# Scratch copies issued from ScalarE's queue, sub-norm rows made by TensorE transposes, zero-padded queries written by GpSimd, small buffers as rings inside one tile

## The chip, the cores and the metric

The kernel runs on one core of a Trainium2 chip. The metric is device time in microseconds of one launch, the median of several runs. Before the change it is 1522.74 us (three runs, 1522.72 to 1524.1).

## What is computed

Two decoder layers over 1040 tokens (16 learned ones and 1024 of the input) of width 1024, in float32. One projection gives the inputs of two groups of attention heads: four differential heads (two softmaxes of 64-wide rotated queries and keys, the second subtracted with a factor, a 128-wide value, then an RMS norm over those 128 channels) and eight forgetting heads (a running sum of log-sigmoids is added to the scores). Both are gated and go through an output projection.

```python
u = rms_norm(h, norm_g)
proj = jnp.einsum('bld,dp->blp', u, w_in)            # dq dk dv dz fq fk fv fz f_logit
...
p = probs(qa, k1) - lam * probs(qc, k2)              # differential heads, q and k after rope
o_a = rms_norm(einsum(p, v_a), subln_g) * (1.0 - lambda_init)
...
s = einsum(q, k_f) * f_scale + c_q - cum             # forgetting heads
mixed = concatenate([o_a * silu(dz), o_b * silu(fz)])
return h + jnp.einsum('blm,md->bld', mixed, w_out)
```

## The kernel before

Every float32 product is made of products of float32r parts: an operand is split into a high part (a cast) and a low part (the rest), and three matmuls stand for one. Token rows are kept transposed in `XTh` and `XTl`, channels on the partitions.

The work of a layer is eight units: units 0 to 3 are the differential heads, units 4 to 7 pairs of forgetting heads. For unit j+1 the program writes `unit_proj` (keys, queries, values; weights are loaded by SyncE, split by GpSimd in `load_w`, L307 and L310, and multiplied at L334) behind `attend` of unit j, and the gates and the norm of unit j behind that. A scheduler then puts each engine's instructions into one fixed order, so that projections of the next unit fill TensorE between the score, transpose and value matmuls of the present one. Each engine, and each engine's DMA queue, works through its list in that order: an instruction that waits holds what stands behind it.

All DMAs are begun by SyncE, through `dma` (L141) and `load_w` (L301). Four kinds matter here:

- the rotary swap: ScalarE writes `raw` out of PSUM (L484), four DMAs copy its 32-row quarters crosswise into `sw`, and VectorE and GpSimd multiply and add (L493 to L495);
- copies of the queries' high part into the other half of the same tile (`qa<-qa`), and of the keys of the forgetting heads (`k<-k`, named k2 in the code);
- the zero-padded low queries of the differential heads: `low_queries` copies 64 rows of `ql` per half and block into `qzs`, two slots behind `XTl` (so the rows name it `XTl<-ql`); it is the stationary operand of the score matmul at L673;
- the norm of the differential heads, `sub_norm`: 1/rms of every token, in `vr`, goes to DRAM (`rr`), comes back broadcast over the partitions (`bc`), and VectorE multiplies the head's output `OT` by it (L901).

Small buffers come from pools (`sm`, and the tags es and ck of `big`). The tile pools are laid out in SBUF by a packer.

Of the kernel before, what the change touches and what calls it, by code (L numbers as in the profile page):

```python
# [12 lines left out]
F32 = mybir.dt.float32  # L13
# [13 lines left out]
NV = 2 * P + 8  # L27
PADC = (272, 544, 1056)
CSW = 1060
LE = max(L, 4 * NV)  # L30
# [4 lines left out]
NE = 4  # L35
ECL = ((272, 4),)
TLS = True
# [14 lines left out]
WLB = 6  # L52
VPB = 2
STB = 3
NQZ = 2
PMB = 4
OTB = 2
CKB2 = 2
Q2B = 2
# [57 lines left out]
def hybrid_kernel(ctx: ExitStack, tc: tile.TileContext, x, meta, norm_g, w_in, b_forget,  # L117
# [40 lines left out]
    def et(name, w=L):  # L158
        for i, (wmax, nb) in enumerate(ECL):
            if w <= wmax:  # L160
                return big.tile([P, wmax], F32, name=name, tag=f"es{i}" if i else "es", bufs=nb or None)
        return big.tile([P, LE], F32, name=name, tag="e", bufs=NE or None)
# [4 lines left out]

    cst = const.tile([P, max(CSW, P + 96 + MW // 2)], F32, name="cst")
    ident = cst[:, 0:P]
# [71 lines left out]
    def rms_stats(hbs, junk, eng):  # L241

        ss = sm.tile([P, 4, 4], F32, name="ss", tag="ss", bufs=3)
# [100 lines left out]
    def load_v01(l):  # L344
# [3 lines left out]
        his, los = room("vwh"), room("vwl")  # L348
        wf = wp.tile([P, KT, 8], F32, name="wf", tag="wf", bufs=1)
        dma(wf, w_in[l, :, 4096:4104].rearrange("(k p) c -> p k c", p=P))  # L350
# [15 lines left out]
    def proj_v01(l, his, los):  # L366
        Vs = [vp.tile([P, NB, 2, P], F32R, name="V", tag="V") for _ in range(2)]
        Vms = [vp.tile([96, 2, P], F32R, name="Vm", bufs=2) for _ in range(2)]
        vpre[l] = (Vs[1], Vms[1])

        mm = big.tile([P, 384], F32R, name="mm", tag="ck", bufs=CKB2 or None).rearrange("p (k c) -> p k c", k=KT)
        nc.gpsimd.memset(mm.bitcast(F32), 0.0)
# [7 lines left out]
        vm = big.tile([P, 384], F32, name="vm", tag="ck", bufs=CKB2 or None)[0:NM, :NV]  # L380
        nc.scalar.copy(vm, ps[32:32 + NM, :NV])
        nc.vector.tensor_tensor(out=vm, in0=ps[0:NM, :NV], in1=vm, op=ALU.add)
        for u in range(2):
# [4 lines left out]
            nc.vector.tensor_tensor(out=Vm[32:32 + NM], in0=x, in1=Vm[0:NM].bitcast(F32), op=ALU.subtract)  # L388
        fn = sm.tile([P, 8, NB], F32, name="fn", tag="fn", bufs=1)
        fm = sm.tile([NM, 8], F32, name="fm", tag="fm", bufs=1)  # L390
        nc.vector.tensor_tensor(out=fm, in0=vm[:, 2 * P:], in1=bfb[0:NM, l], op=ALU.add)
# [22 lines left out]
    def forget(l):  # L414
# [7 lines left out]
        NS = L // 16  # L422
        F = big.tile([P, NM + 2 * P], F32, name="fg", tag="es", bufs=ECL[0][1] or None)
        X, E, T, G = (F[:, i * NS:(i + 1) * NS] for i in range(4))
        off = F[:, 4 * NS:4 * NS + 1]
        tri = big.tile([P, NM + 2 * P], F32, name="tri", tag="es", bufs=ECL[0][1] or None)[:, 0:P]
        tri3 = tri.rearrange("p (a b) -> p a b", b=16)
# [36 lines left out]
    def unit_proj(l, j, U, tabs):  # L464
# [8 lines left out]
        def project(col, chunks, t_lo, scale, split):  # L473
# [9 lines left out]
            def ev(ps, t0, n):  # L483
                nc.scalar.activation(raw[:, t0:t0 + n], ps[:, :n], AF.Copy, scale=scale)  # L484
                todo.append((t0, n))
                if t0 + n < L and len(todo) < RCH:
                    return
                a0, n = todo[0][0], sum(x[1] for x in todo)
                todo.clear()
                c = slice(a0, a0 + n)  # L490
                for a, b in ((0, 32), (32, 0), (64, 96), (96, 64)):
                    dma(sw[a:a + 32, c], raw[b:b + 32, c])
                nc.vector.tensor_tensor(out=raw[:, c], in0=raw[:, c], in1=tabs[0][:, c], op=ALU.mult)  # L493
                nc.gpsimd.tensor_tensor(out=sw[:, c], in0=sw[:, c], in1=tabs[1][:, c], op=ALU.mult)  # L494
                (nc.gpsimd if "a" in ENG else nc.vector).tensor_tensor(out=raw[:, c], in0=raw[:, c], in1=sw[:, c], op=ALU.add)  # L495
                split(raw, a0, 1.0, a0, n)
# [44 lines left out]
        def split_q(src, c0, scale, t0, n):  # L541
# [16 lines left out]
        if not diff and not KE:  # L558
            U.Kb = []
            for m in range(2):  # L560
                k2 = q2t("k2")
                dma(k2[0:64], U.K1[m][halves[m]])
                dma(k2[64:68], augk[:, 2 * (j - 4) + m])
# [13 lines left out]
        V4 = V.rearrange("p b a (c d) -> p b (a c) d", d=64)  # L577
        Vm = vp.tile([96, 2, P], F32R, name="Vm", bufs=2)

        def evv(ps, t0, n):  # L580
            vr = big.tile([P, 384], F32, name="vr", tag="ck", bufs=CKB2 or None)
            nc.scalar.activation(vr[:, :n], ps[:, :n], AF.Copy, scale=1.0 if diff else 0.5)
# [45 lines left out]
    def unit_gate(l, U, from_dram):  # L628
# [9 lines left out]
        def evz(ps, t0, n):  # L638
            gt = big.tile([P, 384], F32, name="gt", tag="ck", bufs=CKB2 or None)
            nc.scalar.activation(gt[:, :n], ps[:, :n], AF.Tanh, scale=0.5)  # L640
# [6 lines left out]
    def low_queries(U, t):  # L647
# [5 lines left out]
        for m in range(2):  # L653
            h = slice(64 * m, 64 * m + 64)
            dma(qz[h, m, :], U.ql[h, t:t + P])
        return [qz[:, m, :] for m in range(2)]

    def scores(U, m, i, low):
# [6 lines left out]
        chs = [(c * n0, n0 if c < nch - 1 else W - c * n0) for c in range(nch)]  # L665
        s = sm.tile([P, 8], F32, name="sst", tag="sst", bufs=SSB or None)
        E = et("E", W)
# [115 lines left out]
    def attend_meta(U):  # L783

        s = sm.tile([P, 8], F32, name="sst", tag="sst", bufs=SSB or None)
        pm2 = ptp.tile([P, 256], F32, name="pm2", tag="pm")[0:16, 0:192].rearrange("p (m c) -> p m c", m=2)
# [28 lines left out]
    def attend(U):  # L815
        U.OT = big.tile([P, L], F32, name="OT", tag="ot", bufs=OTB or None)
        if U.diff:
            U.vr = sm.tile([P, 3, 12], F32, name="vr_", tag="subn", bufs=2)
            if U.l == 0:
# [68 lines left out]
    def sub_norm(U):  # L888
# [84 lines left out]
    for l in range(DEPTH):  # L973
# [59 lines left out]
        if l == 0:  # L1033

            mm = big.tile([P, 384], F32R, name="mm", tag="ck", bufs=CKB2 or None).rearrange("p (k c) -> p k c", k=KT)
            nc.gpsimd.memset(mm.bitcast(F32), 0.0)
# [15 lines left out]
        def out_open(b):  # L1052
# [109 lines left out]
```

## Time and profile before

| | us |
|---|---|
| median of 3 runs | 1522.74 |
| the profiled execution, its own time | 1519.45 |
| its span in the trace | 1517.7 |
| TensorE busy in the span | 1426.1 |
| mean granted TensorE clock, share of full speed | 0.975 |

The span is cut at the stages: up to about 96 us the input is read, normalised and the first projections are made; 96 to 460 us are the differential heads of layer 0; 460 to 670 us its forgetting heads; 670 to 850 us its output projection and the start of layer 1; 850 to 1180 us the differential heads of layer 1; 1180 to 1420 us its forgetting heads; the rest is the last output projection. A stage in which TensorE is busy for the whole stretch can be shortened only by taking work from TensorE; where it is not, one asks what ended each idle time.

### The profile page before, as it was taken

The numbers are of one execution on the slowest core, as the hardware profiler recorded it, in microseconds if no ns is written. First come the engines' busy times: TensorE is split into PE (matmuls) and PEld (weight loads), VectorE is DVE, ScalarE is ACT, GpSimd is POOL, SyncE is SP. The second block draws the span as 40 slices with busy tenths as digits, with TensorE's granted clock in tenths as the row PEclk, the third lists the DMA queues.
The fourth block names the chain that finished last, engine by engine and source line by source line (L and its number), as shares of the span: only waits on it lengthen the run. The fifth ranks groups of instructions, "written<-read, shape, count | busy, mean of one in ns | idle before, by whom it ended". The sixth has DMA issues, their size and how long they took to land.

```text
span 1517.7 us, 26880 instructions
## 1 busy us (share of the span) xinstructions
PE 1426.1 (94%) x9218; PEld 1353.4 (89%) x9218; DVE 966.1 (64%) x2729; ACT 697.7 (46%) x1729; POOL 581.4 (38%) x985
## 2 busy tenths in 40 slices
PE   3999988989899999999999998989898999999997
PEld 3998878989899999997789998889798999999886
DVE  6558684948465756575655686677566466756653
ACT  4236443626444655465323554445344455555521
POOL 6514243523344444464005233343333454535500
PEclk7999999999999999999999999999999999999999
DMA  8325232444133324356424244233433223244632
GB/s 191 66 51 76 33 96 47 87 55 93 25 101 65 62 50 65 93 148 183 135 102 96 40 68 73 55 76 64 61 70 81 68 50 82 45 83 122 208 132 84
DMA packets 132761, 128.37 MB, mean 85 GB/s; under 512 B 26192, under 2 KB 112336, under 8 KB 132624
## 3 DMA queue, kind: packets, MB, share of 16 engines
q1 hardware_dynamic: 132624, 126.65, 38.2%
q8 instruction: 73, 1.20, 0.3%
q14 instruction: 64, 0.52, 0.1%
HBM read 75.15 MB, written 21.57 MB: 64 GB/s over the span
## 4 chain that ended last, share of the span: by engine, by line
PE 69%; DMA 11%; DVE 10%; issue 4%; ACT 3%; POOL 2%; SPq 1%; DVEq 0%; ACTq 0%; POOLq 0%
PE pj L334 34%; PE pss L1049 4%; PE pj L1049 4%; DMA wraw<-in_w_in_dram 3%; PE pss L671 3%; PE pss L673 3%; PE pt L846 3%; PE pj L399 3%; PE po L780 2%; PE po L781 2%; DVE E L677 2%; DMA hb<-in_x_dram 1%; DMA bc<-rr 1%; DVE k L501 1%; PE po L778 1%
## 5 line engine op out<-in xcount | busy, mean ns | idle before, releaser
L334 PE MATMUL pj<-XTh,whi 128*128 128x346 f32 (+5 forms) x1392 | 456.4, 331 | 15.4 <-POOL whi L307 13.6
L334 PE MATMUL pj<-XTl,whi 128*128 128x346 f32 (+5 forms) x1392 | 454.5, 327 | 6.0 <-DVE XTl L286 6.0
L334 PE MATMUL pj<-XTh,wlo 128*128 128x346 f32 (+5 forms) x1392 | 455.5, 328 | 1.7 <-POOL wlo L310 1.7
L684 ACT ACTIVATE E<-E,sst 128x144 f32<-128x144 f32 (+7 forms) x256 | 202.1, 790 | 197.0 <-DVE sst L677 185.3
L334 PEld LDWEIGHTS pj<-XTh,whi 128*128 128x128 f32 x1392 | 265.6, 192 | 19.6 <-POOL whi L307 15.5
L334 PEld LDWEIGHTS pj<-XTl,whi 128*128 128x128 f32 x1392 | 266.1, 191 | 7.4 <-DVE XTl L286 6.4
L334 PEld LDWEIGHTS pj<-XTh,wlo 128*128 128x128 f32 x1392 | 266.5, 192 | 4.5 <-POOL wlo L310 3.6
L307 POOL TENSOR_SCALAR whi<-wraw 128x256 fp32r<-128x256 f32 x232 | 110.1, 475 | 346.4 <-DMA wraw<-in_w_in_dram 315.6
L310 POOL TENSOR_TENSOR wlo<-wraw,whi 128x256 fp32r<-128x256 f32 x232 | 181.0, 781 | 114.8 <-PE pj L334 97.7
L755 DVE TENSOR_TENSOR ptl<-pt,pth 128x512 fp32r<-128x512 f32 (+1 forms) x240 | 147.4, 633 | 52.5 <-ACT pth L754 47.0
L671 PE MATMUL pss<-k,qa 128*128 128x400 f32 (+7 forms) x448 | 154.1, 347 | 10.7 <-DVE sst L677 8.6
L754 ACT CAST pth<-pt 128x512 fp32r<-128x512 f32 (+1 forms) x240 | 122.7, 546 | 85.0 <-PE pt L846 29.8
L677 DVE CUSTOM_DVE_ANT_0 E<-pss,cst 128x400 f32<-128x400 f32 (+7 forms) x256 | 123.9, 491 | 40.6 <-PE pss L673 34.2
L701 POOL TENSOR_SCALAR E<-E,sst 128x400 f32<-128x400 f32 (+7 forms) x128 | 97.2, 762 | 136.2 <-DVE sst L700 121.2
L677 DVE CUSTOM_DVE_ANT_0 E<-pss,cst,sst 128x264 f32<-128x264 f32 (+2 forms) x192 | 112.1, 584 | 36.9 <-PE pss L673 31.9
L671 PEld LDWEIGHTS pss<-k,qa 128*128 128x128 f32 x448 | 86.0, 192 | 16.9 <-DVE sst L677 13.2
L846 PE MATMUL pt<-cst,E 128*128 128x128 f32 x576 | 89.8, 274 | 0.5 <-DVE sst L677 0.5
L780 PE MATMUL po<-pth,V 128*128 128x256 f32 x320 | 84.0, 286 | 0.6 <-POOL pth L865 0.6
L781 PE MATMUL po<-ptl,V 128*128 128x256 f32 x320 | 82.7, 287 | 0.0
L673 PE MATMUL pss<-k,XTl 128*128 128x400 f32 (+6 forms) x224 | 73.4, 334 | 4.0 <-DMA XTl<-ql 4.0
L494 POOL TENSOR_TENSOR sw<-sw,sin 128x694 f32<-128x694 f32 (+3 forms) x32 | 50.1, 1570 | 65.0 <-DMA sw<-raw 51.3
L673 PE MATMUL pss<-k,q 68*128 68x400 f32 (+6 forms) x224 | 72.8, 328 | 0.0
(337 smaller groups left out, 2881.3 us busy)
## 6 DMA issues: line engine op xcount, KB each, us to landing
wraw<-in_w_in_dram SPq DMA_DIRECT2D x256, 128.0 KB
hb<-in_x_dram SPq DMA_DIRECT2D x16, 512.0 KB
wor<-in_w_out_dram SPq DMA_DIRECT2D x64, 128.0 KB
XTl<-ql SPq DMA_DIRECT2D x136, 32.0 KB
sw<-raw SPq DMA_DIRECT2D x48, 86.8 KB
ms<-OT SPq DMA_DIRECT2D x8, 520.0 KB
k<-k SPq DMA_DIRECT2D x16, 260.0 KB
h<-hb SPq DMA_DIRECT2D x8, 512.0 KB
```

The source lines that it names most:

```text
L310: nc.gpsimd.tensor_tensor(out=lo, in0=raw, in1=hi.bitcast(F32), op=ALU.subtract)
L334: nc.tensor.matmul(ps[:, :n], lhsT=w, rhs=xx[:, k, t0:t0 + n], start=(cnt == 0), stop=(cnt == 23))
L671: nc.tensor.matmul(ps[:, :nn], lhsT=U.Qa[m][:, t:t + P], rhs=U.K1[m][:, c0:c0 + nn], start=True, stop=False)
L673: nc.tensor.matmul(ps[:, :nn], lhsT=low[m], rhs=U.Kb[m][:, c0:c0 + nn], start=False, stop=True)
L677: nc.vector.tensor_tensor_reduce(out=E[:, c0:c0 + n], in0=ps[:, :n], in1=k, scale=-1.0, scalar=s[:, c - 1:c] if CHN and c else -NEG, op0=A ...
L684: nc.scalar.activation(E[:, :W], E[:, :W], AF.Exp, scale=-1.0, bias=lo, accum_out=s[:, 4:5])
L754: nc.scalar.copy(hi, ps)
L755: nc.vector.tensor_tensor(out=lo, in0=ps, in1=hi.bitcast(F32), op=ALU.subtract)
L780: nc.tensor.matmul(o[:, :256], lhsT=U.V[:, kb, hd, :], rhs=hi, start=False, stop=False)
L781: nc.tensor.matmul(o[:, :256], lhsT=U.V[:, kb, hd, :], rhs=lo, start=False, stop=last)
L846: nc.tensor.transpose(ps[:, (2 * a + b) * P:(2 * a + b + 1) * P], PP[:, k0:k0 + P], ident)
L1049: nc.tensor.matmul(ps, lhsT=xx[:, k, m0:m0 + P], rhs=wo[k][w][:, c], start=(k == 0 and i == 0), stop=(k == KT - 1 and i == 2))
```

## The change

1. `dma_a` begins the four swap copies, `qa<-qa` and `k<-k` in ScalarE's queue instead of SyncE's: 128 + 48 + 16 DMAs, all of data that ScalarE has just written.
2. `sub_norm` has no DMA any more: TensorE transposes each column of 1/rms, broadcast along the free dimension, into PSUM (9 transposes a head in layer 0, 8 in layer 1, 68 in all), and VectorE multiplies `OT` by PSUM in pieces of 512 columns.
3. The padded low queries are written by GpSimd (`tensor_scalar` times 1, 64 x 128, 136 of them) instead of 136 DMAs, and have three slots instead of two.
4. Small buffers become rings at fixed columns of the constant tile `cst` (so rows of the changed program name them `cst`); `mm` moves to the ring of `pth`; pads of the pools are multiples of 264 elements; the counts of the pools `vp` and `stk` are left to the packer.

```diff
-PADC = (272, 544, 1056)
+PADC = (264, 528, 1056, 2112)
-VPB = 2
-STB = 3
-NQZ = 2
+VPB = 0
+STB = 0
+AQC = True
+NQZ = 3
...
+    def dma_a(dst, src):
+        (nc.scalar if AQC else nc.sync).dma_start(out=f32(dst), in_=f32(src))
...
+    small = [("es", 4, 272), ("ck", 2, 384), ("subn", 2, 36), ("sst", SSB, 8), ("ss", 3, 16), ("fn", 1, 64), ("fm", 1, 8), ("wf", 1, 64)]
+    cst = const.tile([P, P + 96 + MW // 2 + sum(n * w for _, n, w in small)], F32, name="cst")
...
+    def slot(nm):
+        r = rings[nm]
+        c = r[0] + r[3] % r[1] * r[2]
+        r[3] += 1
+        return cst[:, c:c + r[2]]
...
                 for a, b in ((0, 32), (32, 0), (64, 96), (96, 64)):
-                    dma(sw[a:a + 32, c], raw[b:b + 32, c])
+                    dma_a(sw[a:a + 32, c], raw[b:b + 32, c])
...
-                dma(k2[0:64], U.K1[m][halves[m]])
+                dma_a(k2[0:64], U.K1[m][halves[m]])
...
-                dma(U.Qa[m][halves[1 - m], c], U.Qa[m][halves[m], c])
+                dma_a(U.Qa[m][halves[1 - m], c], U.Qa[m][halves[m], c])
...
-            dma(qz[h, m, :], U.ql[h, t:t + P])
+            nc.gpsimd.tensor_scalar(out=qz[h, m, :], in0=U.ql[h, t:t + P].bitcast(F32), scalar1=1.0, scalar2=1.0,
+                                    op0=ALU.mult, op1=ALU.mult)
...
-        row = rr[U.l][U.j]
-        if U.l == 0:
-            dma(row[0:NM].rearrange("(p b) -> p b", b=1), U.vr[0:NM, 1, 0:1])
-        dma(row[NM:].rearrange("(b p) -> p b", p=P), U.vr[:, 1, 1:9])
-        bc = st("bc")
-        dma(bc[:, tq:], bcast_rows(row[tq:], P))
-        nc.vector.scalar_tensor_tensor(out=OT[:, tq:], in0=OT[:, tq:], scalar=gsc[:, U.l, U.j:U.j + 1],
-                                       in1=bc[:, tq:], op0=ALU.mult, op1=ALU.mult)
+        for t0, n, cols in ((0, NM, (0,)), (NM, 4 * P, (1, 2, 3, 4)), (NM + 4 * P, 4 * P, (5, 6, 7, 8))):
+            if t0 < tq:
+                continue
+            ps = pt()
+            w = min(n, P)
+            for i, c in enumerate(cols):
+                nc.tensor.transpose(ps[:, w * i:w * i + w], U.vr[0:w, 1, c:c + 1].to_broadcast([w, P]), ident[0:w, 0:w])
+            o = OT[:, t0:t0 + n]
+            nc.vector.scalar_tensor_tensor(out=o, in0=o, scalar=gsc[:, U.l, U.j:U.j + 1], in1=ps[:, :n],
+                                           op0=ALU.mult, op1=ALU.mult)
```

The scheduler makes the order of every engine anew. SyncE's queue at the norm of head 3 of layer 0, before (`rr_3` and `bc` are the round trip, `wraw` are weights of the next units):

```order
L301 DMA wraw<-in_w_in_dram 128x2x128 x5
L141 DMA rr_3_118<-vr__3863 128x8x1
L141 DMA rr_3_118<-vr__3863 16x1
L141 DMA bc<-rr_3_118 128x1040
L301 DMA wraw<-in_w_in_dram 128x2x128 x2
L141 DMA q_5428<-augq 4x1040
L141 DMA ms_107<-OT 128x1040
L301 DMA wraw<-in_w_in_dram 128x2x128
```

The same place in SyncE's queue of the changed program, where `ms_103<-OT` stores the finished head 3 (the numbers of names differ between the programs):

```order
L313 DMA wraw<-in_w_in_dram 128x2x128 x4
L138 DMA q_4353<-ql 64x1040
L138 DMA q_4354<-ql 64x1040
L313 DMA wraw<-in_w_in_dram 128x2x128
L138 DMA ms_103<-OT 128x1040
L313 DMA wraw<-in_w_in_dram 128x2x128 x11
```

The weights are left nearly alone in this queue: of its 861 instructions that the listing counts 513 stay.

VectorE at the same norm, before: L901 waits for `bc`, and the subtraction for the value matmuls (L770), the score evictions (L677) and the splits (L755) stand behind it.

```order
L700 RECIPROCAL sst<-sst 128x1 x2
L750 TENSOR_TENSOR OT<-po,otmp 64x16
L901 SCALAR_TENSOR_TENSOR OT<-OT,gsc,bc 128x1040
L770 TENSOR_TENSOR pm<-pt,pm 32x256
L677 ISA E,sst<-pss,cst 128x456
```

VectorE there in the changed program: the last step of 1/rms (L249), and then the multiplications by what TensorE put into `pt`.

```order
L249 SCALAR_TENSOR_TENSOR cst<-cst 128x9
L916 SCALAR_TENSOR_TENSOR OT<-OT,gsc,pt 128x16
L614 TENSOR_TENSOR Vm<-vt,Vm 64x128
L630 TENSOR_TENSOR V<-vt,V 128x2x128
L916 SCALAR_TENSOR_TENSOR OT<-OT,gsc,pt 128x512 x2
```

The wait for a DMA is now a wait for transposes that stand between projections in TensorE's order.

ScalarE at the queries of head 1 of layer 0, before (`raw` is written at L484, the exponentials are L684):

```order
L484 ACTIVATE raw<-pj_128_1647 128x346
L484 ACTIVATE raw<-pj_128_1686 128x346
L684 ACTIVATE E,sst<-E,sst 128x784
L763 CAST pm<-pt 32x256
L764 CAST pm<-pt 32x256
L754 CAST pth<-pt 128x384
L684 ACTIVATE E,sst<-E,sst 128x784
```

ScalarE there in the changed program (`raw` is written at L496, the exponentials are L697):

```order
L496 ACTIVATE raw<-pj_128_1601 128x346
L697 ACTIVATE E,cst<-E,cst 128x784
L142 DMA sw<-raw 32x694 x3
L697 ACTIVATE E,cst<-E,cst 128x784
L142 DMA sw<-raw 32x694
L729 COPY OT<-po 128x256
L736 ACTIVATE sq<-po 128x128 x2
L697 ACTIVATE E,cst<-E,cst 128x912
```

Three of the four copies now stand between two exponentials.

## Rows read from the trace of the kernel before

**Rows 1.** The page: busy time of each engine over the span.
```profile
PE 1426.1 (94%) x9218; PEld 1353.4 (89%) x9218; DVE 966.1 (64%) x2729; ACT 697.7 (46%) x1729; POOL 581.4 (38%) x985
```

**Rows 2.** Busy time by stretch: differential, forgetting, and differential heads of layer 1.
```profile
core 0: us, PE busy (x) PEld busy (x) DVE busy (x) ACT busy (x) POOL busy (x), PEclk, DMA share, GB/s
...
96.00:460.00 364.00, 333.74 (x2169) 317.84 (x2168) 247.75 (x733) 174.10 (x452) 133.13 (x220) 0.97 0.35 66
460.00:670.00 210.00, 209.68 (x1471) 206.90 (x1470) 128.36 (x398) 108.82 (x273) 102.57 (x198) 1.00 0.39 79
...
850.00:1180.00 330.00, 303.25 (x1995) 292.66 (x1994) 227.05 (x639) 157.73 (x388) 121.08 (x205) 0.97 0.37 67
```

**Rows 3.** Timeline at head 3's norm, layer 0: start, duration, instruction, [idle before].
```profile
406.35 1.04 SPq L141 DMA_DIRECT2D rr<-vr__3863  x2
...
414.19 0.35 SPq L141 DMA_DIRECT2D bc<-rr  x1
...
418.97 1.30 DVE L901 SCALAR_TENSOR_TENSOR OT<-OT,gsc,bc 128x1040 f32<-128x1040 f32 x1 [7.52 <-DMA bc<-rr]
419.48 1.06 POOL L307 TENSOR_SCALAR whi<-wraw 128x256 fp32r<-128x256 f32 x1 [7.22 <-DMA wraw<-in_w_in_dram]
...
420.77 0.58 PE L758 MATMUL po<-pm,Vm 96*128 96x256 f32 x1 [7.39 <-DVE pm L770]
```

**Rows 4.** Timelines of SyncE, GpSimd and TensorE at head 1's norm, layer 1.
```profile
990.96 0.34 SPq L141 DMA_DIRECT2D bc<-rr  x1
991.39 0.39 SPq L301 DMA_DIRECT2D wraw<-in_w_in_dram  x1
...
993.97 0.40 POOL L307 TENSOR_SCALAR whi<-wraw 128x256 fp32r<-128x256 f32 x1 [11.85 <-DMA wraw<-in_w_in_dram]
...
994.42 0.42 PE L334 MATMUL pj<-XTh,whi 128*128 128x348 f32 x1 [3.99 <-POOL whi L307]
```

**Rows 5.** Busy time around the eight norms, columns as in rows 2; four and the sum.
```profile
192.00:200.10 8.10, 4.10 (x14) 3.32 (x14) 6.67 (x12) 2.37 (x8) 5.91 (x5) 0.79 0.42 104
...
413.00:425.40 12.40, 5.01 (x21) 4.73 (x20) 6.24 (x15) 2.80 (x7) 3.74 (x6) 0.72 0.42 134
...
1072.00:1084.20 12.20, 5.17 (x21) 4.52 (x20) 6.10 (x18) 1.97 (x7) 5.48 (x11) 0.72 0.55 87
1143.00:1152.40 9.40, 4.94 (x22) 4.02 (x21) 3.50 (x10) 1.25 (x3) 2.41 (x4) 0.82 0.50 134
sum 75.40, PE 38.03 PEld 32.62 DVE 33.88 ACT 13.66 POOL 30.59; mean PE 4.75 PEld 4.08 DVE 4.24 ACT 1.71 POOL 3.82
```

**Rows 6.** Line L141, SyncE's DMA issues: nanoseconds min/median/max, first and last start.
```profile
L141 SPq DMA_DIRECT2D sw<-raw x128: 507/586/1961, 55.1 to 1040.4; - x128
...
L141 SPq DMA_DIRECT2D qa<-qa x48: 461/500/688, 77.5 to 1326.6; - x48
```

**Rows 7.** Groups by line, TensorE: busy us, mean ns of one, idle before.
```profile
L846 PE MATMUL pt<-cst,E 128*128 128x128 f32 x576 | 89.8, 274 | 0.5 <-DVE sst L677 0.5
```

**Rows 8.** Waits over the whole span: us in total, times, longest.
```profile
POOL whi L307 <- DMA wraw<-in_w_in_dram: 315.6, 121, 11.8
...
POOL sw L494 <- DMA sw<-raw: 51.3, 19, 7.8
...
DVE raw L493 <- DMA sw<-raw: 22.8, 10, 7.1
```

**Rows 9.** Groups by line and shape, GpSimd, columns as in rows 7.
```profile
L865 POOL MEMSET pth<- 128x128 f32 x96 | 18.7, 205 | 41.8 <-PE po L780 28.3 <-PE po L777 11.0 <-PE po L781 1.3
...
L701 POOL TENSOR_SCALAR E<-E,sst 128x144 f32<-128x144 f32 x16 | 6.2, 385 | 10.4 <-DVE sst L700 6.2 <-DVE vr__3863 L237 4.2
```

**Rows 10.** Groups by line, VectorE, columns as in rows 7.
```profile
L641 DVE SCALAR_TENSOR_TENSOR gt<-gt,pj 128x346 f32<-128x346 f32 (+3 forms) x48 | 24.4, 509 | 27.8 <-ACT gt L640 27.5
...
L901 DVE SCALAR_TENSOR_TENSOR OT<-OT,gsc,bc 128x1040 f32<-128x1040 f32 (+1 forms) x8 | 10.3, 1293 | 61.8 <-DMA bc<-rr 61.8
```

More of the change, by code (lines that the diff above doesn't have):

```diff
@@ L35 @@
 NE = 4
-ECL = ((272, 4),)
 TLS = True
@@ L158, in et @@
     def et(name, w=L):
-        for i, (wmax, nb) in enumerate(ECL):
-            if w <= wmax:
-                return big.tile([P, wmax], F32, name=name, tag=f"es{i}" if i else "es", bufs=nb or None)
+        if w <= 272:
+            return slot("es")
         return big.tile([P, LE], F32, name=name, tag="e", bufs=NE or None)
@@ L165, in q2t @@
         return big.tile([P, L], dt, name=name, tag="q2", bufs=Q2B or None)
-    cst = const.tile([P, max(CSW, P + 96 + MW // 2)], F32, name="cst")
+    small = [("es", 4, 272), ("ck", 2, 384), ("subn", 2, 36), ("sst", SSB, 8), ("ss", 3, 16), ("fn", 1, 64), ("fm", 1, 8), ("wf", 1, 64)]
+    cst = const.tile([P, P + 96 + MW // 2 + sum(n * w for _, n, w in small)], F32, name="cst")
+    rings, at = {}, P + 96 + MW // 2
+    for nm, n, w in small:
+        rings[nm] = [at, n, w, 0]
+        at += n * w
+    def slot(nm):
[3 more added lines that the diff above has]
+        return cst[:, c:c + r[2]]
     ident = cst[:, 0:P]
@@ L241, in rms_stats @@
     def rms_stats(hbs, junk, eng):
-        ss = sm.tile([P, 4, 4], F32, name="ss", tag="ss", bufs=3)
+        ss = slot("ss").rearrange("p (a b) -> p a b", a=4)
         m = len(hbs)
@@ L348, in load_v01 @@
         his, los = room("vwh"), room("vwl")
-        wf = wp.tile([P, KT, 8], F32, name="wf", tag="wf", bufs=1)
+        wf = slot("wf").rearrange("p (k c) -> p k c", k=KT)
         dma(wf, w_in[l, :, 4096:4104].rearrange("(k p) c -> p k c", p=P))
@@ L367, in proj_v01 @@
         Vs = [vp.tile([P, NB, 2, P], F32R, name="V", tag="V") for _ in range(2)]
-        Vms = [vp.tile([96, 2, P], F32R, name="Vm", bufs=2) for _ in range(2)]
+        Vms = [vp.tile([P, 2, P], F32R, name="Vm")[0:96] for _ in range(2)]
         vpre[l] = (Vs[1], Vms[1])
-        mm = big.tile([P, 384], F32R, name="mm", tag="ck", bufs=CKB2 or None).rearrange("p (k c) -> p k c", k=KT)
+        mm = ptp.tile([P, 512], F32R, name="mm", tag="pth", bufs=PHB or None)[:, :384].rearrange("p (k c) -> p k c", k=KT)
         nc.gpsimd.memset(mm.bitcast(F32), 0.0)
@@ L379, in proj_v01 @@
                                  start=(k == 0 and i == 0), stop=(k == KT - 1 and i == 1))
-        vm = big.tile([P, 384], F32, name="vm", tag="ck", bufs=CKB2 or None)[0:NM, :NV]
+        vm = slot("ck")[0:NM, :NV]
         nc.scalar.copy(vm, ps[32:32 + NM, :NV])
@@ L388, in proj_v01 @@
             nc.vector.tensor_tensor(out=Vm[32:32 + NM], in0=x, in1=Vm[0:NM].bitcast(F32), op=ALU.subtract)
-        fn = sm.tile([P, 8, NB], F32, name="fn", tag="fn", bufs=1)
-        fm = sm.tile([NM, 8], F32, name="fm", tag="fm", bufs=1)
+        fn = slot("fn").rearrange("p (h b) -> p h b", h=8)
+        fm = slot("fm")[0:NM]
         nc.vector.tensor_tensor(out=fm, in0=vm[:, 2 * P:], in1=bfb[0:NM, l], op=ALU.add)
@@ L422, in forget @@
         NS = L // 16
[L423 removed]
+        F = slot("es")
         X, E, T, G = (F[:, i * NS:(i + 1) * NS] for i in range(4))
         off = F[:, 4 * NS:4 * NS + 1]
[L426 removed]
+        tri = slot("es")[:, 0:P]
         tri3 = tri.rearrange("p (a b) -> p a b", b=16)
@@ L577, in unit_proj @@
         V4 = V.rearrange("p b a (c d) -> p b (a c) d", d=64)
-        Vm = vp.tile([96, 2, P], F32R, name="Vm", bufs=2)
+        Vm = vp.tile([P, 2, P], F32R, name="Vm")[0:96]
         def evv(ps, t0, n):
-            vr = big.tile([P, 384], F32, name="vr", tag="ck", bufs=CKB2 or None)
+            vr = slot("ck")
             nc.scalar.activation(vr[:, :n], ps[:, :n], AF.Copy, scale=1.0 if diff else 0.5)
@@ L638, in evz @@
         def evz(ps, t0, n):
-            gt = big.tile([P, 384], F32, name="gt", tag="ck", bufs=CKB2 or None)
+            gt = slot("ck")
             nc.scalar.activation(gt[:, :n], ps[:, :n], AF.Tanh, scale=0.5)
@@ L665, in scores @@
         chs = [(c * n0, n0 if c < nch - 1 else W - c * n0) for c in range(nch)]
-        s = sm.tile([P, 8], F32, name="sst", tag="sst", bufs=SSB or None)
+        s = slot("sst")
         E = et("E", W)
@@ L783, in attend_meta @@
     def attend_meta(U):
-        s = sm.tile([P, 8], F32, name="sst", tag="sst", bufs=SSB or None)
+        s = slot("sst")
         pm2 = ptp.tile([P, 256], F32, name="pm2", tag="pm")[0:16, 0:192].rearrange("p (m c) -> p m c", m=2)
@@ L817, in attend @@
         if U.diff:
-            U.vr = sm.tile([P, 3, 12], F32, name="vr_", tag="subn", bufs=2)
+            U.vr = slot("subn").rearrange("p (a b) -> p a b", a=3)
             if U.l == 0:
@@ L1060, in out_open @@
             u = st("u")[:, :D]
-            ss = sm.tile([P, 4, 4], F32, name="ss", tag="ss", bufs=3)
+            ss = slot("ss").rearrange("p (a b) -> p a b", a=4)
             return b, hb, u, ss
```

14 lines of the change are left out of this document (5 added, 9 removed).

## The prediction

> **What bounds the kernel now.** I read the page first, for which engine is full: TensorE is busy 94% of the span, ScalarE 46%, GpSimd 38% [rows 1]. So the time is TensorE's work plus what keeps TensorE waiting, and the next view is busy time by stretch, to see where it waits. In the forgetting heads it is busy 209.7 of 210 us: nothing but less TensorE work shortens those. In the differential heads it is busy 333.7 of 364 us and 303.3 of 330 us, that is 30.3 + 26.7 = 57.0 us idle, and the granted clock is 0.97 there instead of 1.00 [rows 2]. Those 57 us, and what the lower clock takes beside them, are all that an edit of waits can win in these stages.
>
> Then the timeline, for what ended these idle times. At the norm of head 3, 1/rms leaves for DRAM at 406.35; SyncE can begin the way back only at 414.19, when the first has landed; VectorE has stood 7.52 us when it starts L901 at 418.97. What stands behind L901 in its list is late with it, first the subtraction for the value matmul, and TensorE has a gap of 7.39 us at 420.77. GpSimd stood 7.22 us for weights at the same time, because they are behind `bc` in SyncE's queue [rows 3]. At head 1 of layer 1 the second way alone does it: `bc` holds SyncE until 990.96, the weights behind it are begun at 991.39, GpSimd has waited 11.85 us for its next piece, and TensorE 3.99 us for GpSimd [rows 4]. There are eight such norms, and the stretches around them tell what they cost: in 75.4 us TensorE is busy 38.0, so 37.4 of the 57.0 us of idle time lie here. The clock column gives the rest: length times the share not granted is 1.7 us in the first, 3.5 and 3.4 in the two with the long gaps, 1.7 in the last, and 1.7 in each of the four not shown: together 17.1 us [rows 5]. That is the time at the 1.2 GHz level turned into time lost; a part of it was idle anyway, so it is an upper bound.
>
> **The norm without DMAs.** Both the hold on VectorE and the hold on SyncE go: after the change no DMA stands between 1/rms and `OT`. At most 37.4 + 17.1 = 54.5 us return; at least nothing, if the engines then meet another wait at once. VectorE is busy about 70% of these stages and must catch up on what the gap delayed, so I take three quarters: **-41 us**. What it adds: 68 transposes of 128 columns. The group of like transposes takes 89.8/576 = 0.156 us each when they follow each other, 0.274 alone [rows 7]: 10.6 to 18.6 us. Most come in fours and eights, so **+11 us**; it is paid in full, since TensorE has no idle time left to hide it if the gaps go. VectorE pays the same as before: one L901 takes 1.29 us; two pieces of 512 columns out of PSUM, by the multiplication with a PSUM operand of 346 columns at 0.51 us [rows 10], are an estimated 1.4 us. The DRAM trips were 20 DMAs of SyncE, worth nothing but their waits.
>
> **Copies from ScalarE's queue.** An issue held SyncE 0.586 us in the median for a swap, 0.500 for `qa<-qa` [rows 6]; no row shows what one holds ScalarE. With SyncE's price, and that of `qa` for `k<-k` too, it is 128 x 0.586 + 64 x 0.500 = 107 us on an engine now busy 697.7 us. ScalarE is busy 174.1 + 157.7 of 694 us in the differential heads [rows 2]; about 91 us of the new load fall there, which makes 61%. So it fits beside TensorE, but in bits of 0.586, up to 2.3 us for four, and behind such a four stand exponentials and PSUM evictions that others wait for. If TensorE's work queued ahead covers all of it, the cost is nothing; if every swap is paid by TensorE, 75 us. Today TensorE has few short waits besides the eight gaps (57.0 - 37.4 = 19.6 us in two stages), so cover is good: I take 0.3 us for each of the 32 fours, **+10 us**. On the other side stands what the swap no longer waits for: GpSimd waited 51.3 us and VectorE 22.8 us for `sw` behind other DMAs [rows 8]. TensorE felt little of it; **-3 us**, between 0 and the 19.6.
>
> The Trainium skill, DMA: Bandwidth & Descriptors, in Issuing engines are not separate DMA queues, speaks against this part: DMAs begun by several engines run on the same 16 DMA engines, so that a second issuing engine saves only issue time. This trace agrees that bandwidth isn't short (the DMA share is 0.35 and 0.37 in these stages [rows 2]). By the rule alone the moved copies would be worth 0, against my +7 for both sides together.
>
> **Padded queries by GpSimd.** 136 pieces of 64 x 128. No such instruction stands in the trace; the nearest are a memset of 128 x 128 at 0.205 us and a multiplication of 128 x 144 at 0.385 us [rows 9]. At 0.3 us, nearer the second since it reads as well, it is 41 us on an engine with some 440 idle us in those two stages, hidden unless GpSimd stands before it: it waits 315.6 us in 121 pieces for weights, 2.6 us each [rows 8]. Three slots let it work ahead. Between 0 and 52 us (all 136 in the open at 0.385); I take **+3 us**. SyncE is rid of 136 issues.
>
> **Rings, pads and counts** I cost at nothing: the rings have as many places as the pools had (es four, ck two, ss three, sst eight), the same operations run on them, and what covers a late slot is that three to eight are in turn. The price without that cover is one instruction's wait, half a microsecond.
>
> **Sum.** 1519.45 - 41 + 11 + 10 - 3 + 3 = 1499.5 us for an execution like the profiled one. The median of the runs stands 3.3 us above that one (1522.74 against 1519.45), so the forecast is **1502.7, rounded 1503 us**. A measurement here can tell 0.2%, 3 us, from no change.
>
> **Rivals.**
> 1. *The wait only moves.* VectorE, freed of `bc`, meets the next late thing: ScalarE's exponentials or GpSimd's weights (of the 315.6 us of waits for weights the eight norms explain only some). Then a third of the 54.5 us returns, 18: 1519.45 - 18 + 11 + 10 - 3 + 3 + 3.3 = 1526 us. Against it: in the timelines the releasers are `bc` and the weights behind it, by 7.5 and 11.9 us [rows 3, 4].
> 2. *ScalarE's queue holds TensorE.* Place: the swaps, in the stages where exponentials and evictions stand behind them. Without that term the sum is 1492.7; it becomes slower than before when the 32 fours cost TensorE over 30 us, 0.94 us each, two fifths of their 2.3 us. At half it is 1530 us, at the full price 1568. For it: ScalarE works in order, and a copy begun by ScalarE must wait for ScalarE's own last write; against it its 39% of idle time.
> 3. *GpSimd's pieces are late* behind the weights: one wait of 2.6 us for half of the 68 blocks would be 88 us; the three slots speak against it. Only a small part fits: 1515 to 1530 us.
> 4. *The moved copies change nothing.* The DMA share in these stages is 0.35 to 0.37 [rows 2], so no transfer gets faster, and if ScalarE's issues are covered too, the sum is 1519.45 - 41 + 11 + 3 + 3.3 = 1496 us. This is what the section of the Trainium skill named above would make of it.
>
> **Chances.** The forecast, 1480 to 1516 us: 0.50. Rival 4, 1488 to 1500: 0.10, inside it. More than I credit, 1472 to 1480, when all 54.5 us return: 0.07. Rival 1, 1516 to 1530: 0.16; rival 2, over 1526: 0.13; rival 3: 0.04. From this, faster by over 0.2% (under 1519.7) 0.70, within it (to 1525.8) 0.11, slower 0.19. The low end of the range is the upper bounds of gain with the rest as taken, 1519.45 - 54.5 + 11 + 3.3 = 1479, less some of the 19.6 us: 1473; the high end is rival 2 at half its price, 1530. The likeliest case alone spans 1480 to 1516.
>
> **What would show it.** Right: no gap of over 3 us ends at a norm, the differential stages are busy over 96% at a clock of 0.99, and are some 12 us shorter each in layer 0 and 1. The transposes: about 0.16 us each in a row, none waiting over 0.5 us for 1/rms. ScalarE's issues: each about 0.5 to 0.6 us in its queue, and no TensorE gap that ends with an exponential or eviction behind a swap. GpSimd's pieces at 0.2 to 0.4 us, with no score matmul waiting for them. Wrong: new gaps in the differential heads whose releaser is ScalarE, or GpSimd's padded queries; or differential stages as long as before though the gaps at the norms are gone.

## The result, and the profile after

| | before | after |
|---|---|---|
| median, four runs each | 1523.16 us | 1502.03 us (1499.49 to 1505.8) |
| ratio, 95% interval | | 0.9862 [0.9839, 0.9886] |
| profiled execution, span | 1517.7 us | 1501.8 us |

The change makes the kernel 1.4% faster, 21.1 us, where 20 were forecast (1503 us). The page of the changed kernel, to be held against [rows 1]:

```profile
PE 1429.4 (95%) x9286; PEld 1357.7 (90%) x9286; DVE 968.8 (65%) x2741; ACT 701.0 (47%) x1729; POOL 637.6 (42%) x1121
```

The 68 transposes stand in TensorE's count, the 136 pieces in GpSimd's, 56 us of work more. Next the stretches of the eight norms, each 11 us from shortly ahead of L916, VectorE's multiplication by 1/rms; columns as in [rows 2], first and last and the sum:

```profile
188.00:199.00 11.00, 10.43 (x66) 9.68 (x67) 9.40 (x24) 5.12 (x14) 6.76 (x11) 1.00 0.47 89
...
1128.00:1139.00 11.00, 11.00 (x76) 10.77 (x75) 8.59 (x26) 5.78 (x13) 5.42 (x12) 1.00 0.18 60
sum 88.00, PE 83.66 PEld 78.79 DVE 61.84 ACT 34.17 POOL 53.16; mean PE 10.46 PEld 9.85 DVE 7.73 ACT 4.27 POOL 6.64
```

and stretches of the same length around the norms of the kernel before (there, ahead of L901):

```profile
191.00:202.00 11.00, 7.00 (x34) 6.07 (x33) 8.57 (x15) 3.39 (x9) 8.07 (x8) 0.84 0.48 142
...
415.00:426.00 11.00, 5.23 (x22) 5.23 (x23) 6.79 (x16) 2.23 (x5) 4.04 (x6) 0.69 0.53 173
...
sum 88.00, PE 55.71 PEld 50.65 DVE 52.56 ACT 21.49 POOL 45.99; mean PE 6.96 PEld 6.33 DVE 6.57 ACT 2.69 POOL 5.75
```

TensorE's idle time at the norms falls from 32.3 to 4.3 us, and its granted clock there, 0.69 to 0.84 before (six stretches at 0.84, two at 0.69, which makes 17.4 us lost of 88), is 1.00 in all eight. At the norms themselves the change does what was promised: 28.0 us of idle time and at most 17.4 us of clock, 45 us by this count (at most, because the clock was low in a part of the idle time too). TensorE's timeline at head 2's norm in layer 1 (the gap of 7.39 us in [rows 3] was at another norm, head 3's in layer 0):

```profile
1061.03 0.31 PE L346 MATMUL pj<-XTh,wlo 128*128 128x340 f32 x1
1061.18 1.03 PE L914 MATMUL pt<-cst 128*128 128x128 f32 x8
1061.97 0.41 PE L346 MATMUL pj<-XTl,whi 128*128 128x340 f32 x1
```

Eight transposes take about 1 us between two projection matmuls, and nothing stands still. The whole of the two layers' heads, cut at the last value projection before them and at the last value matmul, tells how much of the 45 us is left; the kernel after, layer 0 and layer 1:

```profile
97.10:683.20 586.10, 559.35 (x3759) 538.91 (x3758) 397.01 (x1167) 296.51 (x752) 267.45 (x491) 0.99 0.35 70
847.10:1404.60 557.50, 546.84 (x3747) 538.09 (x3746) 379.74 (x1081) 288.65 (x693) 259.38 (x474) 0.98 0.33 66
```

and the kernel before:

```profile
95.20:684.20 589.00, 558.42 (x3738) 539.54 (x3738) 389.75 (x1162) 294.46 (x751) 244.51 (x429) 0.98 0.37 72
844.00:1420.10 576.10, 548.78 (x3721) 536.02 (x3721) 377.55 (x1080) 288.29 (x697) 234.23 (x418) 0.98 0.36 72
```

Layer 1 is 18.6 us shorter, layer 0 only 2.9. Idle time in both fell from 57.9 to 37.4 us, though 28.0 left the norms: 7.5 us came back in other places, as short waits. Of the clock more came back: summed over slices of 5 us, the share not granted cost about 22 us in these heads before and costs about 15 now, so some 7 of the 17.4 us stay gone. Together that is 27 of the 45 us. TensorE's waits over the whole span of the changed kernel (us in total, times, longest) say which:

```profile
PE pt L287 <- DVE u L272: 19.2, 4, 15.5
PE pss L684 <- DVE cst L690: 11.2, 9, 3.1
PE pj L346 <- POOL whi L319: 3.9, 4, 1.3
PE po L771 <- DVE pm L783: 3.4, 3, 1.5
```

The first is the start of the kernel. The rest are waits of one to three us, for VectorE's reading of scores (L690), GpSimd's weights (L319) and VectorE's part for the value matmul (L783); none waits for a transpose or for 1/rms. But two dips of the clock lie right behind the first two norms of layer 0:

```profile
199.00:215.00 16.00, 12.01 (x60) 10.71 (x60) 14.12 (x30) 7.99 (x19) 10.02 (x16) 0.79 0.29 82
285.00:299.00 14.00, 9.95 (x56) 9.36 (x57) 8.53 (x22) 5.37 (x14) 7.14 (x16) 0.88 0.45 87
```

TensorE is idle 8.0 us in these two stretches, and their clock costs another 5. What ends its waits there is VectorE and GpSimd (L756, L602, L783 and L322), and they are late behind instructions that take longer than elsewhere: the last section shows those of the first stretch.

### The profile page after: what moved, and what is told of

Its sections match the earlier page's. It is cut to its first block, busy times and chain, and to the rows that moved or that the text cites. A ratio compares the mean times of both kernels' runs of the same rounds, so it can differ in the third digit from the quotient of the medians.

```text
span 1501.8 us, 26868 instructions
## 1 busy us (share of the span) xinstructions
PE 1429.4 (95%) x9286; PEld 1357.7 (90%) x9286; DVE 968.8 (65%) x2741; ACT 701.0 (47%) x1729; POOL 637.6 (42%) x1121
## 5 line engine op out<-in xcount | busy, mean ns | idle before, releaser
L690 DVE CUSTOM_DVE_ANT_0 E<-pss,cst 128x346 f32<-128x346 f32 (+6 forms) x384 | 211.3, 558 | 64.4 <-PE pss L686 41.7
L697 ACT ACTIVATE E<-E,cst 128x400 f32<-128x400 f32 (+2 forms) x192 | 172.3, 897 | 138.6 <-DVE cst L690 130.1
L319 POOL TENSOR_SCALAR whi<-wraw 128x256 fp32r<-128x256 f32 x232 | 103.6, 447 | 260.8 <-DMA wraw<-in_w_in_dram 199.0
L322 POOL TENSOR_TENSOR wlo<-wraw,whi 128x256 fp32r<-128x256 f32 x232 | 182.0, 785 | 70.4 <-PE pj L346 49.0
L684 PE MATMUL pss<-k,qa 128*128 128x400 f32 (+7 forms) x448 | 149.6, 338 | 12.2 <-DVE cst L690 11.2
L714 POOL TENSOR_SCALAR E<-E,cst 128x400 f32<-128x400 f32 (+2 forms) x96 | 85.5, 891 | 90.6 <-DVE cst L713 84.4
L684 PEld LDWEIGHTS pss<-k,qa 128*128 128x128 f32 x448 | 85.7, 191 | 17.8 <-DVE cst L690 15.0
L667 POOL TENSOR_SCALAR XTl<-ql 64x128 fp32r<-64x128 f32 x136 | 56.1, 418 | 94.0 <-PE pss L686 60.6
L859 PE MATMUL pt<-cst,E 128*128 128x128 f32 x576 | 85.8, 274 | 1.8 <-DVE cst L756 0.9
L686 PE MATMUL pss<-k,q 68*128 68x400 f32 (+6 forms) x224 | 73.3, 330 | 0.0
L686 PE MATMUL pss<-k,XTl 128*128 128x400 f32 (+6 forms) x224 | 71.7, 326 | 0.6 <-POOL XTl L667 0.6
L859 PEld LDWEIGHTS pt<-cst,E 128*128 128x128 f32 x576 | 68.0, 141 | 4.6 <-DVE cst L690 1.4
```

What stands on the lines that cost most here:

```text
L319: nc.gpsimd.tensor_scalar(out=hi, in0=raw, scalar1=1.0, scalar2=1.0, op0=ALU.mult, op1=ALU.mult)
L322: nc.gpsimd.tensor_tensor(out=lo, in0=raw, in1=hi.bitcast(F32), op=ALU.subtract)
L684: nc.tensor.matmul(ps[:, :nn], lhsT=U.Qa[m][:, t:t + P], rhs=U.K1[m][:, c0:c0 + nn], start=True, stop=False)
L686: nc.tensor.matmul(ps[:, :nn], lhsT=low[m], rhs=U.Kb[m][:, c0:c0 + nn], start=False, stop=True)
L690: nc.vector.tensor_tensor_reduce(out=E[:, c0:c0 + n], in0=ps[:, :n], in1=k, scale=-1.0, scalar=s[:, c - 1:c] if CHN and c else -NEG, op0=A ...
L697: nc.scalar.activation(E[:, :W], E[:, :W], AF.Exp, scale=-1.0, bias=lo, accum_out=s[:, 4:5])
```

## The experiments

All were timed in five rounds, four kernels on one chip beside the kernel before. The changed kernel was not timed again beside them, so the last column, the ratio's distance from its 0.9862 times 1520 us, carries the uncertainty of two ratios, 4 to 5 us. A scheduler orders every build anew, so each experiment also has another order of instructions; where that could be counted, it is given as the number of TensorE's instructions that stand in the same order in two kernels.

| run | what it is | us | ratio, interval | to the change |
|---|---|---|---|---|
| u_norm | norm by DMA again | 1525.98 | 1.0022 [1.0008, 1.0036] | +24 |
| u_copies | copies from SyncE again | 1505.65 | 0.989 [0.9872, 0.9909] | +4 |
| u_queries | padded queries by DMA again | 1492.55 | 0.9805 [0.9785, 0.9825] | -9 |
| rings_only | all three of these | 1544.42 | 1.0147 [1.0124, 1.0169] | +43 |
| r_cnt | rings_only, old counts | 1530.94 | 1.0087 [1.0065, 1.0109] | +34 |
| r_padc | rings_only, old widths | 1520.8 | 1.0017 [1.0004, 1.0031] | +24 |
| dbl_transposes | each transposition twice | 1506.79 | 0.993 [0.9906, 0.9955] | +10 |
| dbl_copies | each swap copy twice | 1483.29 | 0.9769 [0.9744, 0.9794] | -14 |
| a_padc | change, old widths | 1504.77 | 0.991 [0.9886, 0.9934] | +7 |
| q_padc | u_queries, old widths | 1491.1 | 0.9817 [0.9794, 0.984] | -7 |
| a_nqz | change, two query places | 1583.11 | 1.0424 [1.04, 1.0448] | +85 |
| dbl_queries | each query piece twice | 1520.79 | 1.0015 [0.9999, 1.0031] | +23 |

### Undoing one part at a time

The norm goes back through DRAM, with the lines of before:

```diff
-        for t0, n, cols in ((0, NM, (0,)), (NM, 4 * P, (1, 2, 3, 4)), (NM + 4 * P, 4 * P, (5, 6, 7, 8))):
...
+        row = rr[U.l][U.j]
+        dma(row[NM:].rearrange("(b p) -> p b", p=P), U.vr[:, 1, 1:9])
+        bc = st("bc")
+        dma(bc[:, tq:], bcast_rows(row[tq:], P))
```

> The changed kernel with 1/rms sent through DRAM again, all else as changed. My theory (41 us of stalls and lower clock at the eight norms come back, 11 us of transposes go): about 1532. The rival that the wait only moves (18 us come back, 11 go): about 1509. If the norm's edit was worth nothing, 1502.

It measured 24 us slower than the changed kernel. Its waits show the hold again, and TensorE's busy time in eight stretches of 11 us around L915 is 59.63 of 88 us:

```profile
DVE OT L915 <- DMA bc<-rr: 55.6, 8, 9.6
...
sum 88.00, PE 59.63 PEld 55.68 DVE 61.36 ACT 28.82 POOL 48.24; mean PE 7.45 PEld 6.96 DVE 7.67 ACT 3.60 POOL 6.03
```

So the norm is the part that carries the gain, by these rows more than by the 24 us, since under three fifths of TensorE's instructions in the two traces stand in the same order. That the wait would only move falls: undoing it would then have cost 7 us, 1509.

The copies go back to SyncE:

```diff
-AQC = True
+AQC = False
```

> The changed kernel with the swap, query and key copies back in SyncE's queue, all else as changed. My theory (issues on ScalarE cost TensorE about 10 us, the swaps that no longer stand behind other DMAs give 3 back): 7 us less than the changed kernel's 1502, about 1495. The rival that the moved copies change nothing, since the same 16 DMA engines run them: 1502, within 3. The rival that taking them out of SyncE's queue is itself a gain: over 1506, with longer waits of GpSimd for the weights and for the swapped tile.

It did not get faster by 7 us. That it is slower, by some 4 us, isn't shown: the two intervals overlap, and by the two traces only a little over a third of TensorE's instructions stand in the changed kernel's order. So ScalarE's issues cost nothing that can be seen. GpSimd waits 43.1 us for `sw` there, 22.8 in the changed kernel.

```profile
POOL sw L506 <- DMA sw<-raw: 43.1, 19, 5.7
```

TensorE also stands 14.6 us in two waits for `qa<-qa` here, the first before any head, and in the changed kernel for none. SyncE's queue alone is not the reason: the next kernel, with these copies in ScalarE's queue, has the same two waits, 16.0 us.

The padded queries go back to DMAs, with three places kept:

```diff
-            nc.gpsimd.tensor_scalar(out=qz[h, m, :], in0=U.ql[h, t:t + P].bitcast(F32), scalar1=1.0, scalar2=1.0,
-                                    op0=ALU.mult, op1=ALU.mult)
+            dma(qz[h, m, :], U.ql[h, t:t + P])
```

> The changed kernel with the padded low queries copied by SyncE's DMAs again, three slots kept. My theory (GpSimd's pieces cost TensorE 3 us): 1499. The rival that they are late behind the weights: 1490 or less. The rival that 136 DMAs in SyncE's queue are the worse choice, since weights stand behind them: over 1506.

It got 9 us faster, and beats both kernels; neither the theory nor its first rival gave this time. In the heads of its two layers (columns as above) TensorE is idle 11.5 and 5.6 us, where the changed kernel has 26.8 and 10.7:

```profile
110.60:673.50 562.90, 551.40 (x3788) 537.01 (x3787) 383.74 (x1171) 293.10 (x748) 238.14 (x428) 1.00 0.37 71
845.90:1386.80 540.90, 535.33 (x3725) 526.42 (x3724) 367.22 (x1075) 284.53 (x686) 234.13 (x415) 1.00 0.35 71
```

These 20 us less are not all gain, since the heads start 13.5 us later here: ahead of them TensorE has one long wait, at 89.17 us, that the changed kernel does not have:

```profile
89.17 0.35 PE L803 MATMUL pss<-k,qa 128*128 128x16 f32 x1 [10.93 <-DMA qa<-qa]
```

With all three undone only the rings, widths, counts and the third query place are left of the change:

> All three moves undone, so that only the rings, the pads, the third query slot and the free pool counts are left of the change. My theory costs these at nothing: as before, 1523 within 3 us. A rival: the rings and pads themselves carry part of the gain (1515 or less) or cost some (over 1528).

That is 22 us slower than the kernel before, from a part that was costed at nothing. The next runs look for these 22 us.

### What the storage part costs

```diff
-VPB = 0
-STB = 0
+VPB = 2
+STB = 3
```

> The kernel with only the storage part of the change (rings, pads, third slot; 1544 us), with the two counts of before put back: two places for V, three for the tiles of a unit's queries and keys. If the free counts are what costs the 22 us, it comes back to 1522 to 1530 us; if the fixed rings in one tile or the pads cost it, it stays at 1540 to 1549.

```diff
-PADC = (264, 528, 1056, 2112)
+PADC = (272, 544, 1056)
```

> The same storage-only kernel (1544 us) with the row widths of before (272, 544, 1056) put back. If the widths cost the time, because they decide which tiles may take one another's room, 1522 to 1530 us; if it is the fixed rings or the counts, 1540 to 1549. Anything between says that the order of instructions that the scheduler happens to find moves the time by itself.

Both got faster, by 9 and by 20 us: together more than the 22 looked for, so they aren't two causes to be added. They differ in a thing that the times don't show: with the old counts 9037 of TensorE's 9106 instructions keep rings_only's order, with the old widths 4489. Most of the counts' 9 us can be placed. From the end of layer 0's heads to the heads of layer 1, rings_only and then r_cnt:

```profile
688.30:861.10 172.80, 165.24 (x900) 141.06 (x898) 91.64 (x223) 55.76 (x141) 45.48 (x64) 0.97 0.41 115
```

```profile
683.90:846.90 163.00, 160.64 (x903) 137.75 (x902) 91.56 (x224) 55.53 (x142) 46.98 (x65) 1.00 0.44 122
```

This one stretch is 9.8 us longer with free counts (the two profiled spans differ by 17.1): 5.2 us more idle and a clock of 0.97 instead of 1.00. The longest of the waits that r_cnt does not have:

```profile
847.70 0.56 PE L412 MATMUL pj<-vwh,XTh 128*128 128x264 f32 x1 [2.85 <-DVE cst L418]
```

TensorE waits until VectorE has read a projection (L418), which it does behind four rotary subtractions (L514), 2.8 us in all; in the 3 us after it, 848 to 851, the granted clock is about 0.5. Why free counts put it so was not looked into. The widths were then tried where they leave the order alone, in the changed kernel and in the one with queries by DMA:

> The changed kernel (0.986 of before) with the row widths of before. Its order of instructions is the changed kernel's almost throughout: 9146 of TensorE's 9174 instructions stand in the same order. If the widths cost time by themselves (who may use whose room), as the storage-only pair seemed to show, 14 to 22 us less, 1480 to 1490 us, 0.972 to 0.978; if those 22 us came from the other order that the scheduler found, no difference: 0.983 to 0.989.

> The changed kernel with its padded queries by DMA (0.9805 of before), with the row widths of before; 9166 of 9174 instructions of TensorE stand in the same order. Widths by themselves: 0.966 to 0.972; the order that was found: 0.978 to 0.983.

Both say that the widths by themselves bring no time back: +7 and +2 us against the same kernel with the new widths, on another chip. The +7 lies outside both forecasts, so a pair in the same order can differ by that much. In these two kernels, then, the widths are not worth 20 us. If the same holds in rings_only, which was not tested with its order kept, r_padc's 20 us come from the other order that the scheduler found (and with it, where the packer puts the tiles), and two orders of the same work differ by 20 us. Most of the storage part's 22 us may be of that kind; about 9 go with the counts, in a pair that nearly keeps its order, and that is little more than the 7 of a_padc.

The third query place is the storage part's other half:

```diff
-NQZ = 3
+NQZ = 2
```

> The changed kernel with two places for the padded queries in place of three: the same instructions, but only 3118 of TensorE's 9174 stand in the same order. If the order is worth little, 0.984 to 0.990, since a place more was costed at nothing; if what order the scheduler finds moves the time by ten or twenty us by itself, it may lie anywhere from 0.975 to 1.00.

With two places the changed kernel is 85 us slower, far outside the forecast. The waits suggest a mechanism, GpSimd's for the matmul (L686) that still reads the place; first this kernel, then the changed one:

```profile
POOL XTl L667 <- PE pss L686: 156.9, 49, 27.7
```

```profile
POOL XTl L667 <- PE pss L686: 60.6, 29, 11.6
```

The pieces now hold GpSimd while they have no place, up to 27.7 us at a time, and the splitting of the next unit's weights stands behind them. That this reaches TensorE isn't shown: of TensorE's waits here, those for the weights are no longer than the changed kernel's 3.9 us.

```profile
PE pj L346 <- POOL whi L319: 3.6, 4, 1.8
```

Nor does the length of GpSimd's wait foretell the time: it is 93.7 us in u_copies, some 4 us from the changed kernel, and 96.5 us in dbl_copies below, which is the fastest of all. And 16.6 us of TensorE's idle time are the two waits for `qa<-qa` that u_copies and u_queries have too. How much of the 85 us is this hold and how much the other order (3118 of 9174 alike) the run does not tell apart; the two are not independent, as the scheduler orders around the places.

### Doubling a suspected cost

```diff
+                for _ in range(2):
                     nc.tensor.transpose(ps[:, w * i:w * i + w], U.vr[0:w, 1, c:c + 1].to_broadcast([w, P]), ident[0:w, 0:w])
```

> Each of the norm's 68 transpositions is written twice (the second does the first's work again). If they are paid in full on TensorE, as in the prediction's sum, 68 x 0.156 = 10.6 us more, 1511 to 1514 us; if they lie in idle time of TensorE, 1500 to 1505.

10 us more, give or take 5. By the groups of TensorE's work (busy us, mean ns; pipelined ones overlap) the transposes are 9.7 us of the changed kernel and 16.6 when doubled:

```profile
L914 PE MATMUL pt<-cst 128*128 128x128 f32 (+1 forms) x68 | 9.7, 270 | 0.1
```

```profile
L915 PE MATMUL pt<-cst 128*128 128x128 f32 (+1 forms) x136 | 16.6, 270 | 1.1 <-ACT raw L496 0.6 <-DVE cst L249 0.4
```

```diff
                     dma_a(sw[a:a + 32, c], raw[b:b + 32, c])
+                    dma_a(dr.tile([32, 1040], F32, name=f"scr{len(scr)}")[:, :n], raw[b:b + 32, c])
```

> Each of the 128 swap copies that ScalarE begins is begun a second time by ScalarE, into scratch memory that nobody reads: 128 x 0.51 = 65 us more of ScalarE held, and no further wait. By the prediction (about 0.3 us of four copies' 2 us reach TensorE, some for the other copies) 7 to 12 us more, 1508 to 1515 us; if ScalarE's held time reaches TensorE by half, about 1535; if ScalarE has room for it, 1500 to 1505.

The kernel that holds ScalarE 128 issues longer is the fastest of all, 14 us below the changed one. No theory here had that sign. Line L142's issues, and what waited for them, say that ScalarE did pay:

```profile
L142 ACTq DMA_DIRECT2D sw<-raw x128: 513/551/1522, 55.0 to 1022.2; - x128
L142 ACTq DMA_DIRECT2D scr<-raw x128: 308/433/1691, 58.5 to 1022.8; - x128
...
  ACT raw L497: 15.1, 3
```

At 803.26 us ScalarE has stood 6.76 us behind such a copy, the longest; the second row is TensorE in the 13 us around it, 12.76 us busy:

```profile
803.26 0.93 ACT L497 ACTIVATE raw<-pj 128x346 f32<-128x346 f32 x2 [6.76 <-DMA scr<-raw]
```

```profile
795.00:808.00 13.00, 12.76 (x83) 12.53 (x82) 3.82 (x5) 3.72 (x7) 9.39 (x14) 1.00 0.62 138
```

So ScalarE's longest stand does not reach TensorE, and in the whole span TensorE waits 0.6 us for line L142. The 14 us must come from elsewhere, since work was only added; 5909 of 9174 instructions stand in the changed kernel's order, and a better order is what is left. That is argued, not shown: a build with this order and without the second copies was not tried.

```diff
+            for _ in range(2):
                 nc.gpsimd.tensor_scalar(out=qz[h, m, :], in0=U.ql[h, t:t + P].bitcast(F32), scalar1=1.0, scalar2=1.0,
                                         op0=ALU.mult, op1=ALU.mult)
```

> Each of GpSimd's 136 query pieces is done twice, 56 us more of GpSimd by the changed kernel's rows (0.418 us each). If the 9.5 us that the kernel with queries by DMA gained are the price of GpSimd's time, as much again: 0.991 to 0.995; if they came from another order, it may lie on either side of 0.986.

23 us more for 136 pieces more, where 8 to 14 were forecast, after 9 us less for 136 pieces less. The sign is that of a price of GpSimd's both times, but neither difference stands far enough above what another order does (4664 and 3277 of 9174 alike) to be that price; both kernels also have the waits for `qa<-qa`, 10.3 and 16.0 us of TensorE.

## Why the prediction came out right, by its steps

**The norm.** Forecast -41 us. At the eight norms 28.0 us of idle time and up to 17.4 us of clock did go, no gap of over 3 us ends at a norm, and undoing it costs 24 us net of its transposes. With their 10 us that is 34 us gross, three quarters of the 45; by the rows of the whole heads 27 of the 45 stay gone, three fifths. The mechanism is right, and the three quarters, a guess, lie near; that undoing gives them so closely is luck, since the order changed with it. Much of what comes back lies in layer 0, which is 2.9 us shorter where some 12 were expected, while layer 1 is 18.6 us shorter. Over the whole heads, which include the forgetting ones, the sign "busy over 96%" holds in layer 1 alone, 546.84 of 557.50 us, 98%, and the clock of 0.99 in layer 0 alone; layer 0 is 95% busy, layer 1's clock 0.98.

**The transposes.** +11 us; by the groups 9.7 us, doubled +10 us. Eight in a row take 1.03 us, 0.13 each, and none of them waits for 1/rms. This term is right. The 0.274 us that the prediction read as the time of one alone is the mean length of one in a group whose members overlap; the upper bound of 18.6 us, which rested on it, played no part.

**ScalarE's issues and the swap.** +10 - 3 = +7 us; mis-sized. The issue price was right, 0.584 and 0.472 us in the median:

```profile
L142 ACTq DMA_DIRECT2D sw<-raw x128: 514/584/1809, 55.8 to 1031.7; - x128
...
L142 ACTq DMA_DIRECT2D qa<-qa x48: 468/472/684, 82.0 to 1314.0; - x48
```

but no price of it shows on TensorE, in u_copies or dbl_copies; the copies are worth 4 us at most by u_copies, within its uncertainty of nothing. Rival 2 is dead; rival 4, that the moved copies change nothing, was nearer than the forecast. The Trainium skill, DMA: Bandwidth & Descriptors, in Issuing engines are not separate DMA queues, says a second issuing engine saves only issue time, usually little; these 4 us, not clear of nothing, do not speak against it.

**GpSimd's queries.** +3 us; probably undersized, 9 us by undoing, 23 by doubling, both with another order. The price of one piece is 0.297 us in the median (the estimate was 0.3), its mean 0.418, and GpSimd waits 60.6 us for places:

```profile
L667 POOL TENSOR_SCALAR XTl<-ql x136: 288/297/1703, 82.9 to 1075.1; 64x128 fp32r<-64x128 f32 x136
...
  PE pss L686: 60.6, 29
```

Two things were missed: GpSimd stands for a free place with the weights behind it (rival 3 had this place, with another cause), and its pieces are stretched (last section): 136 take 56.8 us, where 0.297 each would be 40. GpSimd's idle share says nothing of either. By which of them, if by any, TensorE pays stays open.

**Rings, pads and counts.** Costed at nothing: the step that failed. With only this part the kernel is 22 us slower; some 9 of that go with the free counts, the rest is not settled. And the kernel without the third place, which was taken as cover, is 85 us slower, by the place or by its order.

**The sum** came out 1 us from the measurement because errors cancel: the parts undone singly (24 + 4 - 9 = 19 us gain) and rings_only's loss of 22 do not even add up to the 21 us gained; that each build has its own order is the likely reason. The norm by transposes alone, in the kernel before, was not tried, so what it is worth without the storage part stays open. A term under some 20 us can't be read from one build's total here; the norm's can, because its rows show up to 45 us gone from eight named places.

## What to carry to other kernels

Where a scheduler orders the program anew for each build, compare the order first: an experiment that keeps it (here the widths, 9146 of 9174) prices a part, to 7 us here, and one that changes it prices a part and an order together, an order being worth up to 20 us here if the widths' pair is read rightly. A wait that stands at named places in the trace, as the norm's, can be costed from its rows; "no work, so no cost" did not hold here for places and counts, which change what may run ahead and so the order. Work moved to an engine with idle time was free here where nothing that TensorE needs soon stood behind it (ScalarE's copies); where it can wait for a buffer ahead of someone's weights (GpSimd's queries), look at that wait before trusting the idle share. The fastest version with no needless work is the change with its queries left as DMAs, 0.9805 of before.

## What the hardware showed that was not expected

VectorE's and GpSimd's instructions stretch each other. Of VectorE's subtraction L513 in the changed kernel, the 48 that read PSUM take 511 to 523 ns; the 32 of the same or twice the width with both inputs in SBUF go from 511 to 1504. Width does not explain it: of the 16 that are 694 wide, the four beside which GpSimd runs nothing that reads take 876 to 878 ns, the others up to 1504.

```profile
L513 DVE TENSOR_TENSOR k<-pj,k x48: 511/515/523, 327.1 to 1288.4; 64x346 fp32r<-64x346 f32 x32, 64x348 fp32r<-64x348 f32 x16
L513 DVE TENSOR_TENSOR k<-raw,k x32: 511/876/1504, 70.2 to 1020.0; 64x694 fp32r<-64x694 f32 x16, 64x346 fp32r<-64x346 f32 x16
```

At the same time GpSimd's cast of weights, 0.407 us in the median, takes 1.04 us at 204.44, while VectorE runs two subtractions of this line, 694 wide (`ql<-raw,qa`), in 2.93 us from 202.28, where 1.75 would be two unstretched ones:

```profile
204.44 1.04 POOL L319 TENSOR_SCALAR whi<-wraw 128x256 fp32r<-128x256 f32 x1
205.45 0.81 POOL L667 TENSOR_SCALAR XTl<-ql 64x128 fp32r<-64x128 f32 x2
```

This is the place of the first dip of the clock in layer 0: TensorE's idle times at 203.00 and 207.25 end with a GpSimd subtraction that took 1.00 us (0.74 at its usual) and with VectorE's L756, which stands behind these subtractions.

The Trainium skill, SBUF — State Buffer, in SBUF: two separate sides, says that a VectorE instruction with two inputs in SBUF and a GpSimd instruction that reads SBUF exclude each other for a whole instruction; these rows agree. GpSimd's query pieces are 136 more of the latter kind, but how much of their 9 us comes by this way no run shows.
